# A float32 streaming-encoder step: the last four of sixteen chunks of x brought to feature layout by VectorE's 32x32 block transposes instead of TensorE products with the identity

## The chip, the cores and the metric

The kernel runs on one core of one Trainium2 chip. The metric is device time of the whole program in microseconds (us). Before the change it is 1937.66 us, the median of 3 runs (1937.37 to 1938.39). Every time below comes from those runs or from one profiled execution of the same program.

## What is computed

One layer of a hybrid encoder is run on 384 token rows of width 2048: 256 rows of one new stream (`x_prompt`) and 8 x 16 rows of running streams (`x_sample`). All data are float32. The part of the reference that the change touches is the first norm and the projection that follows it:

```python
def rmsnorm(x, g):
    xf = x.astype(jnp.float32)
    r = xf * lax.rsqrt(jnp.mean(xf * xf, axis=-1, keepdims=True) + EPS)
    return (r * g.astype(jnp.float32)).astype(x.dtype)
...
    h = rmsnorm(x, norm_mix_g)
    proj = h @ w_in
```

`proj` holds the values v, the queries, the keys, the forget logits, the input of a gated convolution branch and two gates. Attention, the convolution branch, an output projection and a feed-forward network with its own norm follow; the change touches none of them.

## The kernel before, in words

**Layout.** The 384 tokens are three tiles of 128 (`NTT = 3`, `NT = 384`), the 2048 features sixteen chunks of 128. x is loaded with tokens on partitions into four tiles `xs[0..3]`, each with 512 features, that is four chunks. A product with `w_in` needs features on partitions, so every chunk c of x is turned into a 128 x 384 block of `hT[c // 4]`. TensorE works in float32 by splitting both operands into a high part (type fp32r) and a low part (the rest): each product is three matmuls, high x high, high x low, low x high (lines 318 to 320 in `gemm`, in that order: L319 reads the low part of the weights, L320 the low part of x).

**Turning a chunk (`x_chunk`, L371 to 379).** TensorE multiplies three 128 x 128 tiles with the identity into one PSUM tile called misc (L374). ScalarE writes the high part of hT from it, scaled by the norm's weight g (L378), and VectorE writes the low part, g times x minus the high part (L379). The factor of the norm that belongs to a token, `rs1`, isn't applied here; it scales the products when they leave PSUM (`tok_evac`, L530 to 537).

**Weights.** `ahead` (L252) keeps two or three units of weights ready. A unit is 256 rows of w_in by up to 512 columns. SyncE's queue starts its DMA into one of three tiles `raw` (L157), ScalarE casts the high part `hi` (L176), VectorE subtracts to get the low part `lo` (L177). A `raw` tile is free for the next fetch only when VectorE's subtraction has read it, so SyncE's next fetch waits for `lo`. In this stage the same queue also starts the loads of x, two chunks at a time (L116, L118).

**The stage of the change.** The first product is for v: `gemm([(v_jobs[0], v_jobs[2])], [norm_steps])`, L542. It goes through the sixteen chunks in eight pairs. For a pair, job 0 uses one unit of weights (344 columns) for chunk c and then c + 1, and job 1 uses the next unit for the same two chunks: 4 x 9 matmuls a pair. After each nine matmuls `tick` advances a side generator, `first_norm` (L478). It calls `x_chunk` for the two chunks of the next pair, after the second and the third of the four ticks, and after each fourth chunk it has ScalarE sum the squares of one `xs` tile (L489, three instructions with the name junk). After the last of these sums VectorE and ScalarE work out `rs1` in a chain of ten small instructions (L500 to 503 and L127 to 132). Then the accumulators of v leave PSUM (L535), which frees the PSUM banks for the next product, the queries.

**What sets the order.** TensorE's order is written out by hand. On the other engines instructions go in the order that the scheduler chose by priority when the program was built: weights (`SPLIT_AHEAD`) and evictions (`EVAC_AHEAD`) go ahead of what has no priority, and `queued` keeps these among themselves in the order of the calls. Each engine then executes its list strictly in order.

Of the kernel before, what the change touches and what calls it, by code (L numbers as in the profile page):

```python
# [8 lines left out]
F32 = mybir.dt.float32  # L9
F32R = mybir.dt.float32r  # L10
AF = mybir.ActivationFunctionType
ALU = mybir.AluOpType
# [3 lines left out]
P = 128  # L16
DM = 2048
NT = 384
# [8 lines left out]
O_A, O_B, O_Q, O_K, O_V, O_GA, O_GB = 0, 1024, 2048, 3072, 4096, 5128, 7176  # L27

ATT_FIRST = 5
CONV_FIRST, CONV_LAG = 24, 17  # L30
LN_LAG = 0
SQ_LAG = 1
# [9 lines left out]
def hybrid_step(  # L42
# [9 lines left out]
    nc = tc.nc  # L52

    def pool(name, side="left", bufs=1, space=None):
        kw = dict(name=name, bufs=bufs, reuse_waits="tile")
        if space is not None:
            kw["space"] = space
        else:
            kw["side"] = side
        cm = tc.tile_pool(**kw)  # L60
        p = cm.__enter__()
        return p, lambda: cm.__exit__(None, None, None)
# [15 lines left out]
    def misc_tile():  # L78
        made[1] += 1
        return misc.tile([P, 512], F32, tag="misc", name="misc")  # L80
# [9 lines left out]
    def f(ap):  # L90
        return ap.bitcast(F32)
# [4 lines left out]
    stt = nc.vector.scalar_tensor_tensor  # L96
# [3 lines left out]
    p_x0, close_x0 = pool("x0", side="left")  # L100
    xs = [p_x0.tile([P, NTT, 512], F32, name=f"xs{n}") for n in range(4)]
# [4 lines left out]
    def queued(d, chain=True):  # L106
        e = d.ins.engine
        if chain and e in newest:
            tc.add_manual_dep(d.ins, newest[e], mybir.DependencyInfo(
                mybir.DependencyClass.NoSync, mybir.DependencyReason.DATA), reason="queue")  # L110
        newest[e] = d.ins.name
# [22 lines left out]
    def rsqrt(m, shape, p, tag):  # L134
        s = p.tile(shape, F32, tag=tag + "s", name=tag + "s")
        r = p.tile(shape, F32, tag=tag + "r", name=tag + "r")
        newton_rsqrt(r[:], s[:], m)
        return r
# [24 lines left out]
    def split_tiles():  # L163
        if banks and wide[0]:
            wide[0] += 1
            if wide[0] % 4 == 1:
                return res["wide"]()
        if extra and len(plan) > after_glu + 2:
            turns[0] += 1
            if turns[0] % 4 == 0:  # L170
                return [extra[0].tile([P, 2, 512], F32R, tag=tag, bufs=1, name=tag) for tag in ("hi", "lo")]
        return [wp.tile([P, 2, 512], F32R, tag=tag, bufs=3, name=tag) for tag in ("hi", "lo")]
# [177 lines left out]
    def by_feature(dst):  # L350
        return lambda a, js: dst[js].rearrange("p m (t a i) -> p m t a i", t=NTT, a=4)[:, :, :, a]
# [12 lines left out]
    hT = [gp.tile([P, 2, 4, NT], F32R, tag=f"G{g}", name=f"hT{g}") for g in range(4)]  # L364

    gm = cp.tile([P, 16], F32, name="gm")
# [4 lines left out]
    def x_chunk(c):  # L371
        ps = misc_tile()
        for t in range(NTT):
            tr(ps[:, t * P:(t + 1) * P], xs[c // 4][:, t, c % 4 * P:(c % 4 + 1) * P], ident[:])  # L374
        g = gm[:, c:c + 1]
        hi, lo = hT[c // 4][:, 0, c % 4, :], hT[c // 4][:, 1, c % 4, :]
        with tc.high_priority(offset=EVAC_AHEAD):
            queued(nc.scalar.activation(hi, ps[:, :NT], AF.Identity, scale=g))  # L378
            queued(stt(lo, ps[:, :NT], g, f(hi), op0=ALU.mult, op1=ALU.subtract))  # L379

    pe_order = tc.manual_schedule(engines={ENG.PE})
    pe_order.__enter__()
    with tc.manual_schedule(engines={ENG.SP, ENG.Activation, ENG.DVE}):
# [20 lines left out]
        hi, lo = split_tiles()  # L404
# [10 lines left out]
    def diagonals(dg, r):  # L415
        for t in range(NTT):
            ts(dg[:, t, :], ident[:], r[:, t:t + 1], None, op0=ALU.mult)
        return dg

    def over_partitions(dg, dst):  # L420
        ps = misc_tile()
        for t in range(NTT):
            mm(ps[:, t * P:(t + 1) * P], ones[:], dg[:, t, :], start=True, stop=True)
        nc.scalar.copy(dst, ps[:, :NT])
# [47 lines left out]
    def small_columns():  # L472
        ps = misc_tile()
        tr(ps[:, :R_N], vrow[:R_N, :], ident[:R_N, :R_N])
        nc.vector.tensor_copy(col[:], ps[:, :R_N])
        ts(qgs[:], col[:, R_QG:R_QG + 1], float(P) ** -0.5, None, op0=ALU.mult)

    def first_norm():  # L478
        for c in range(2, 16, 2):
            if c == 2:  # L480
                yield
            yield
            x_chunk(c)
            yield
            x_chunk(c + 1)
            if c % 4 == 2:
                for t in range(NTT):
                    n = c // 4
                    sq = nc.scalar.activation(junk[:], xs[n][:, t, :], AF.Square, accum_out=ssx[:, t, n:n + 1])  # L489
                    if c == 14:  # L490
                        queued(sq)
                    else:
                        tc.keep_in_program_order(sq)
            if c < 14:
                yield
            if 2 < c < 14:
                yield
        mt = p_x0.tile([P, NTT], F32, name="mt")
        with tc.high_priority(offset=EVAC_AHEAD):
            nc.vector.tensor_reduce(mt[:], ssx[:], axis=mybir.AxisListType.X, op=ALU.add)  # L500
            ts(mt[:], mt[:], 1.0 / DM, EPS, op0=ALU.mult, op1=ALU.add)
            r = rsqrt(mt[:], [P, NTT], p_x0, "r1")
            nc.vector.tensor_copy(rs1[:], r[:])
        for _ in range(14):
            yield
        small_columns()
        yield
        dg = diagonals(p_x0.tile([P, NTT, P], F32, name="r1d"), rs1)
        yield
        yield  # L510
        over_partitions(dg, rs1b[:])
        yield
# [26 lines left out]
    ha = grouped(hT)  # L539
    v_jobs = [job("B", 16, ha, tok_evac(vt, 344 * i, 344, shared=i == 2), n=344) for i in range(3)]  # L540
    norm_steps = first_norm()
    gemm([(v_jobs[0], v_jobs[2])], [norm_steps])  # L542

# [215 lines left out]
    def attention():  # L759
        at = {}  # L760
        for d in heads:
            for off, step in ((1, head_operands), (4, head_scores), (9, head_probs),
                              (12, head_out), (14, head_last)):
                at[ATT_FIRST + 6 * d["h"] + off] = step, d
        for t in range(max(at) + 1):
# [108 lines left out]
    for h in range(H):  # L874
        hi, lo = aHL[h // 4][:, 0, h % 4, :], aHL[h // 4][:, 1, h % 4, :]
# [710 lines left out]
    for n in (2, 3):  # L1586
        t = gp.tile([P, 2, 4, NT], F32R, tag=f"G{5 - n}", name=f"late{n}")
# [79 lines left out]
```

## Time and profile before

| | before |
|---|---|
| median of 3 runs | 1937.66 us |
| the profiled execution | 1938.61 us |
| its span, first to last instruction | 1936.9 us |
| TensorE busy in it | 1928.4 us |
| VectorE busy | 1556.1 us |
| ScalarE busy | 932.5 us |
| granted TensorE clock | 1.00 |

Time zero is the first instruction. The profiled execution took 1938.61 us, 1.7 us more than its span; it stands 0.95 us above the median. PE is TensorE's matmul part and PEld its weight load, which overlaps it; DVE is VectorE, ACT ScalarE, POOL GpSimd, SPq the DMA queue of SyncE. A row of a timeline reads: start, duration, engine, line, operation, output<-inputs, shapes, count, and in brackets the idle time ahead of it and what ended that.

### The profile page before, as it was taken

Reading aid. Unit: us, or ns where it says so; the run is one execution under the profiler, and the core shown is the slowest. Engines: PE = TensorE matmul, PEld = TensorE weight load, DVE = VectorE, ACT = ScalarE, POOL = GpSimd, SP = SyncE. Lnnn points to the kernel's source line nnn. Section 1 sums busy time; section 2 is a strip of 40 time slices with the busy share of each in tenths; the row PEclk is TensorE's granted clock in tenths of the full one; section 3 lists DMA queues with packets and bytes.
Section 4 is the critical chain, followed back from the end, with each engine's and each line's share of the span. In section 5 each row is a group of like instructions: output and inputs, shape, how many; then the busy total and the mean of one; then the engine's idle time right before and its main releaser. Section 6 shows DMA issues by size and latency. Waiting matters only on the chain.

```text
span 1936.9 us, 25423 instructions
## 1 busy us (share of the span) xinstructions
PE 1928.4 (100%) x9132; PEld 1629.3 (84%) x9132; DVE 1556.1 (80%) x2131; ACT 932.5 (48%) x1322; POOL 151.0 (8%) x298
## 2 busy tenths in 40 slices
PE   9999999999999999999999999999999999999999
PEld 9888999988888888888888888888888888888887
DVE  4446979888864568677699989898999999999985
ACT  5444454433333522344556464555555555555552
POOL 2000001100000000000101010101010101101010
PEclk9999999999999999999999999999999999999999
DMA  6564677454444343634545454545454545545453
GB/s 185 156 184 119 211 166 167 136 148 126 132 132 130 121 130 129 205 124 130 154 147 164 145 164 149 153 152 162 133 164 151 165 152 155 166 139 177 134 162 138
DMA packets 220721, 293.37 MB, mean 151 GB/s; under 512 B 59354, under 2 KB 105109, under 8 KB 220587
## 3 DMA queue, kind: packets, MB, share of 16 engines
q1 hardware_dynamic: 213395, 281.74, 49.1%
q0 software_dynamic: 7168, 10.00, 2.0%
q8 instruction: 71, 1.16, 0.3%
q14 instruction: 55, 0.45, 0.1%
q10 hardware_dynamic: 32, 0.01, 0.0%
HBM read 266.98 MB, written 7.86 MB: 142 GB/s over the span
## 4 chain that ended last, share of the span: by engine, by line
PE 96%; DVE 2%; DMA 1%; issue 0%; SPq 0%; ACT 0%; ACTq 0%; DVEq 0%
PE bank L1412 17%; PE bank L1411 17%; PE bank L1410 17%; PE acc L320 8%; PE acc L318 8%; PE acc L319 8%; PE misc L320 4%; PE misc L318 4%; PE misc L319 4%; PE acc L313 2%; PE acc L315 2%; PE acc L314 2%; DMA raw<-in_w_down_dram 0%; DVE mixT L337 0%; DVE lo L177 0%
## 5 line engine op out<-in xcount | busy, mean ns | idle before, releaser
L1103 ACT CAST hi<-raw 128x1024 fp32r<-128x1024 f32 x260 | 270.3, 1051 | 316.1 <-DVE raw L1103 140.3
L177 DVE TENSOR_TENSOR lo<-raw,hi 128x1024 fp32r<-128x1024 f32 (+2 forms) x219 | 259.5, 1187 | 194.7 <-ACT hi L176 192.5
L176 ACT CAST hi<-raw 128x1024 fp32r<-128x1024 f32 (+2 forms) x219 | 221.7, 1012 | 387.9 <-PE misc L320 300.6
L1103 DVE TENSOR_TENSOR lo<-raw,hi 128x1024 fp32r<-128x1024 f32 x260 | 314.7, 1221 | 48.2 <-ACT hi L1103 46.5
L318 PE MATMUL acc<-hi,hT 128*128 128x512 f32 (+1 forms) x512 | 193.1, 377 | 1.3 <-ACT hT L378 1.3
L320 PE MATMUL acc<-hi,hT 128*128 128x512 f32 (+1 forms) x512 | 190.5, 372 | 0.1
L319 PE MATMUL acc<-lo,hT 128*128 128x512 f32 (+1 forms) x512 | 190.1, 371 | 0.0
L1410 PE MATMUL bank<-hi,xg 128*128 128x512 f32 x440 | 171.2, 389 | 0.0
L1411 PE MATMUL bank<-lo,xg 128*128 128x512 f32 x440 | 171.2, 389 | 0.0
L1412 PE MATMUL bank<-hi,xg 128*128 128x512 f32 x440 | 171.2, 389 | 0.0
L835 DVE SCALAR_TENSOR_TENSOR ut<-ext,cw,ut 128x384 f32<-128x384 f32 x240 | 151.2, 630 | 6.0
L1412 PE MATMUL bank<-hi,act 128*128 128x512 f32 x396 | 154.2, 389 | 0.2 <-DVE act L1103 0.2
L1410 PE MATMUL bank<-hi,act 128*128 128x512 f32 x396 | 154.1, 389 | 0.0
L1411 PE MATMUL bank<-lo,act 128*128 128x512 f32 x396 | 154.0, 389 | 0.0
L1103 ACT CAST x21h<-raw 128x1024 fp32r<-128x1024 f32 x82 | 86.2, 1051 | 101.7 <-DVE raw L1103 50.1
L318 PEld LDWEIGHTS acc<-hi,hT 128*128 128x128 f32 x512 | 96.3, 188 | 16.6 <-ACT hT L378 1.6
L320 PEld LDWEIGHTS acc<-hi,hT 128*128 128x128 f32 x512 | 96.1, 188 | 15.5 <-DVE hT L379 0.5
L319 PEld LDWEIGHTS acc<-lo,hT 128*128 128x128 f32 x512 | 96.4, 188 | 14.9
L1103 DVE TENSOR_TENSOR x21l<-raw,x21h 128x1024 fp32r<-128x1024 f32 x82 | 100.2, 1222 | 7.8 <-ACT x21h L1103 6.7
L1411 PEld LDWEIGHTS bank<-lo,xg 128*128 128x128 f32 x440 | 82.6, 188 | 17.1
L1410 PEld LDWEIGHTS bank<-hi,xg 128*128 128x128 f32 x440 | 82.6, 188 | 17.1
L1412 PEld LDWEIGHTS bank<-hi,xg 128*128 128x128 f32 x440 | 82.6, 188 | 17.1
(393 smaller groups left out, 4277.1 us busy)
## 6 DMA issues: line engine op xcount, KB each, us to landing
raw<-in_w_up_dram SPq DMA_DIRECT2D x176, 512.0 KB
raw<-in_w_in_dram SPq DMA_DIRECT2D x96, 512.0 KB
raw<-in_w_down_dram SPq DMA_DIRECT2D x88, 512.0 KB
raw<-in_w_in_dram SPq DMA_DIRECT2D x64, 256.0 KB
raw<-in_w_out_dram SPq DMA_DIRECT2D x32, 512.0 KB
raw<-in_w_att_out_dram SPq DMA_DIRECT2D x16, 512.0 KB
raw<-in_conv_pw_out_dram SPq DMA_DIRECT2D x16, 512.0 KB
raw<-in_w_in_dram SPq DMA_DIRECT2D x23, 344.0 KB
```

The source lines that it names most:

```text
L176: queued(nc.scalar.copy(hi[:, k, :o], raw[:, k, :o]), first)
L177: queued(tt(lo[:, k, :o], raw[:, k, :o], f(hi[:, k, :o]), op=ALU.subtract), first)
L313: mm(o, hi[:, kk, s], ah, start=st, stop=False)
L314: mm(o, hi[:, kk, s], al, start=False, stop=False)
L318: mm(o, ah[:, s], hi[:, kk, :n], start=st, stop=False)
L319: mm(o, ah[:, s], lo[:, kk, :n], start=False, stop=False)
L320: mm(o, al[:, s], hi[:, kk, :n], start=False, stop=sp)
L835: stt(o, v, wc, o, op0=ALU.mult, op1=ALU.add)
L1103: d = op(*args, **kw)
L1410: mm(o, ah, h[:, kk, :], start=start, stop=False, **kw)
L1411: mm(o, ah, l[:, kk, :], start=False, stop=False, **kw)
L1412: mm(o, al, h[:, kk, :], start=False, stop=stop, **kw)
```

## The change

For chunks 12 to 15 `x_chunk` isn't called any more. Instead `x_pair(c)` is called for c = 12 and c = 14, one tick earlier than `x_chunk(c)` was. It has VectorE transpose the two chunks in blocks of 32 x 32 straight from `xs` into a new SBUF tile `xT`: 16 instructions a pair, each reading 32 partitions and writing 32 partitions, with 2 chunks x 3 token tiles x 32 = 192 elements a partition. ScalarE and VectorE then write the high and low part of hT as before, with `xT` in place of the PSUM tile as input. These two are still `queued`, but no longer under `EVAC_AHEAD`, and the transposes have no priority either. The removed matmuls are 4 chunks x 3 = 12.

```diff
@@ -27,6 +27,7 @@
 ATT_FIRST = 5
+X_PAIRS = 12
 CONV_FIRST, CONV_LAG = 24, 17
@@ -377,6 +378,19 @@
+    def x_pair(c):
+        xT = p_x0.tile([P, 2, NT], F32, tag="xT", bufs=2, name="xT")
+        o = c % 4 * P
+        src = xs[c // 4][:, :, o:o + 2 * P].rearrange("p t (m b j) -> p b m t j", m=2, b=4)
+        for b in range(4):
+            for a in range(4):
+                nc.vector.transpose(by_feature(xT)(a, slice(32 * b, 32 * b + 32)), src[32 * a:32 * a + 32, b])
+        for m in range(2):
+            g = gm[:, c + m:c + m + 1]
+            hi, lo = hT[c // 4][:, 0, c % 4 + m, :], hT[c // 4][:, 1, c % 4 + m, :]
+            queued(nc.scalar.activation(hi, xT[:, m], AF.Identity, scale=g))
+            queued(stt(lo, xT[:, m], g, f(hi), op0=ALU.mult, op1=ALU.subtract))
@@ -479,10 +493,14 @@
         for c in range(2, 16, 2):
             if c == 2:
                 yield
+            if c >= X_PAIRS:
+                x_pair(c)
             yield
-            x_chunk(c)
+            if c < X_PAIRS:
+                x_chunk(c)
             yield
-            x_chunk(c + 1)
+            if c < X_PAIRS:
+                x_chunk(c + 1)
             if c % 4 == 2:
```

The lists of the engines that the two programs were built to show what this moves. On TensorE only the twelve matmuls are gone; on SyncE and GpSimd nothing moves. Behind the stretch shown the lists are the same on all engines, but for one small instruction of VectorE that trades places with a weight subtraction. Line numbers of the changed program are larger by 1 up to the end of `x_chunk`, by 14 up to the calls of `x_chunk` in `first_norm` and by 18 behind them.

First place, VectorE, from the low part of chunk 9 on (`lo_...` are low parts of weights, `hT2` holds chunks 8 to 11, `hT3` chunks 12 to 15). Before:

```order
L379 SCALAR_TENSOR_TENSOR hT2_87<-misc_438,gm_89,hT2_87 128x384
L177 TENSOR_TENSOR lo_458<-raw_455,hi_457 128x2x344
L379 SCALAR_TENSOR_TENSOR hT2_87<-misc_479,gm_89,hT2_87 128x384
L177 TENSOR_TENSOR lo_488<-raw_485,hi_487 128x2x344
L379 SCALAR_TENSOR_TENSOR hT2_87<-misc_500,gm_89,hT2_87 128x384
L177 TENSOR_TENSOR lo_523<-raw_520,hi_522 128x2x344
```

After:

```order
L388 STREAM_TRANSPOSE xT_535<-xs3_79 32x6x32 x2
L380 SCALAR_TENSOR_TENSOR hT2_87<-misc_438,gm_89,hT2_87 128x384
L178 TENSOR_TENSOR lo_458<-raw_455,hi_457 128x2x344
L388 STREAM_TRANSPOSE xT_535<-xs3_79 32x6x32 x12
L380 SCALAR_TENSOR_TENSOR hT2_87<-misc_479,gm_89,hT2_87 128x384
L178 TENSOR_TENSOR lo_488<-raw_485,hi_487 128x2x344
L388 STREAM_TRANSPOSE xT_535<-xs3_79 32x6x32
L380 SCALAR_TENSOR_TENSOR hT2_87<-misc_500,gm_89,hT2_87 128x384
```

The first sixteen transposes stand between the low parts of chunks 9 to 11, twelve of them in one block ahead of the low part of chunk 10 and of `lo_488`; the sixteenth follows the last row shown.

Second place, VectorE, from there to the start of the `rs1` chain. Before:

```order
L379 SCALAR_TENSOR_TENSOR hT3_88<-misc_544,gm_89,hT3_88 128x384
L177 TENSOR_TENSOR lo_553<-raw_550,hi_552 128x2x344
L379 SCALAR_TENSOR_TENSOR hT3_88<-misc_565,gm_89,hT3_88 128x384
L177 TENSOR_TENSOR lo_585<-raw_582,hi_584 128x2x344
L177 TENSOR_TENSOR lo_591<-raw_588,hi_590 128x2x344
L379 SCALAR_TENSOR_TENSOR hT3_88<-misc_612,gm_89,hT3_88 128x384
L177 TENSOR_TENSOR lo_621<-raw_618,hi_620 128x2x344
L379 SCALAR_TENSOR_TENSOR hT3_88<-misc_633,gm_89,hT3_88 128x384
```

After:

```order
L388 STREAM_TRANSPOSE xT_612<-xs3_79 32x6x32
L178 TENSOR_TENSOR lo_568<-raw_565,hi_567 128x2x344
L388 STREAM_TRANSPOSE xT_612<-xs3_79 32x6x32 x2
L178 TENSOR_TENSOR lo_594<-raw_591,hi_593 128x2x344
L388 STREAM_TRANSPOSE xT_612<-xs3_79 32x6x32 x6
L178 TENSOR_TENSOR lo_600<-raw_597,hi_599 128x2x344
L388 STREAM_TRANSPOSE xT_612<-xs3_79 32x6x32 x4
L393 SCALAR_TENSOR_TENSOR hT3_88<-xT_612,gm_89,hT3_88 128x384 x2
L178 TENSOR_TENSOR lo_645<-raw_642,hi_644 128x2x344
```

The sixteen transposes of the second pair are mixed with three weight subtractions (the same three as `lo_553`, `lo_585` and `lo_591` before; their numbers changed); the first three of them stand between the rows of the first place and these. The low parts of chunks 14 and 15 now come last but one, behind all 32 transposes.

Third place, ScalarE, the same stretch (`junk` are the sums of squares). Before:

```order
L176 CAST hi_590<-raw_588 128x2x344
L378 ACTIVATE hT3_88<-misc_612,gm_89 128x384
L176 CAST hi_620<-raw_618 128x2x344
L378 ACTIVATE hT3_88<-misc_633,gm_89 128x384
L489 ACTIVATE junk_92,ssx_91<-xs3_79 128x512 x3
L127 ACT_TABLE_LOAD
```

After:

```order
L177 CAST hi_599<-raw_597 128x2x344
L392 ACTIVATE hT3_88<-xT_612,gm_89 128x384 x2
L177 CAST hi_644<-raw_642 128x2x344
L507 ACTIVATE junk_92,ssx_91<-xs3_79 128x512 x3
L128 ACT_TABLE_LOAD
```

The high parts of chunks 14 and 15 stand together now, they wait for VectorE's last transpose, and the cast of a weight unit and the sums of squares that `rs1` needs stand behind them.

## The prediction

> **What bounds the kernel now.** First the page's shares and its chain of work that ended last, then the idle time of TensorE by what ended it:
>
> ```profile
> span 1936.9 us, 25423 instructions
> PE 1928.4 (100%) x9132; PEld 1629.3 (84%) x9132; DVE 1556.1 (80%) x2131; ACT 932.5 (48%) x1322; POOL 151.0 (8%) x298
> ...
> PE 96%; DVE 2%; DMA 1%; issue 0%; SPq 0%; ACT 0%; ACTq 0%; DVEq 0%
> ```
>
> ```profile
> PE misc L398 <- POOL ident L123: 1.5, 1, 1.5
> PE acc L318 <- ACT hT L378: 1.3, 1, 1.3
> PE misc L966 <- DVE sgA L960: 0.5, 2, 0.3
> ```
>
> TensorE bounds the kernel from end to end. Its longest waits are over by 10 us of 1937, and behind them none is longer than 0.3 us. So a microsecond taken off TensorE's stream is a microsecond gained, a microsecond that it newly waits is one lost, and nothing later takes it back. Next the stretch of the change, from the windows of busy time:
>
> ```profile
> 33.15:54.15 21.00, 21.00 (x140) 20.89 (x139) 10.46 (x14) 12.20 (x25) 0.00 (x0) 1.00 0.61 168
> ```
>
> The columns are length, then busy time and count of PE, PEld, DVE, ACT and POOL, then the granted clock. TensorE has no gap in these 21.00 us; VectorE is busy for 10.46 and has 10.54 to spare.
>
> **What the change removes.** Two of the removed turns in TensorE's timeline, with the start of the product pair ahead of them:
>
> ```profile
> 40.23 0.32 PE L318 MATMUL acc<-hi,hT 128*128 128x344 f32 x1
> ...
> 43.07 0.49 PE L374 MATMUL misc<-ident,xs 128*128 128x128 f32 x3
> ...
> 44.81 0.49 PE L374 MATMUL misc<-ident,xs 128*128 128x128 f32 x3
> ```
>
> From 40.23 to 43.07 stand eighteen matmuls of 344 columns: 2.84 / 18 = 0.158 us from start to start. From 43.07 to 44.81 stand one turn and nine such matmuls: 1.74 - 9 x 0.158 = 0.32 us for a turn. Four turns are gone: **-1.29 us**, if everything else holds.
>
> **What it adds.** 32 transposes of 192 elements a partition. The profile has transposes of 384 on 32 partitions, and of 256 on 128:
>
> ```profile
> L337 DVE STREAM_TRANSPOSE attT<-qt 32x384 f32<-32x384 f32 x32 | 18.2, 570 | 0.5
> ...
> L812 DVE STREAM_TRANSPOSE ext<-sc 128x256 f32<-128x256 f32 x8 | 3.5, 439 | 1.8 <-DMA sc<-in_state_conv_dram 1.7
> ```
>
> ```profile
> 146.50 3.49 DVE L337 STREAM_TRANSPOSE attT<-qt 32x384 f32<-32x384 f32 x6
> 150.02 1.23 DVE L177 TENSOR_TENSOR lo<-raw,hi 128x1024 fp32r<-128x1024 f32 x1
> 151.28 4.09 DVE L337 STREAM_TRANSPOSE attT<-qt 32x384 f32<-32x384 f32 x7
> ```
>
> 128 elements fewer cost 131 ns less, so 64 fewer than 256 should cost 65 less: 439 - 65 = 374 ns. Six in a row take 3.49 us, (3.49 - 0.57) / 5 = 0.584 from start to start, 0.014 of it gap. I take **0.384 us** apiece, 12.29 us in all. The bounds are 0.285 (half of 570, no fixed cost) and 0.584 (the wider one's spacing, no saving by width). The form of the access is that of L337 with half the blocks, so I stay near the straight line.
>
> 12.29 us are more than the 10.54 us to spare. So VectorE must become the bound for a while, and the sum has to follow its list. These rows give where it starts and the other two kinds in it:
>
> ```profile
> 31.54 0.62 DVE L379 SCALAR_TENSOR_TENSOR hT<-misc,gm,hT 128x384 fp32r<-128x384 f32 x1 [3.06 <-ACT hT L378]
> 32.20 0.88 DVE L177 TENSOR_TENSOR lo<-raw,hi 128x688 fp32r<-128x688 f32 x1
> 33.29 0.62 DVE L379 SCALAR_TENSOR_TENSOR hT<-misc,gm,hT 128x384 fp32r<-128x384 f32 x1 [0.22 <-ACT hT L378]
> ```
>
> The first transposes take the place of the 0.22 us wait after the row at 32.20, at 32.20 + 0.88 + 0.03 (the gap seen above ahead of 151.28) = 33.11. By the new order these stand up to the last transpose: 32 transposes (12.29), the low parts of chunks 9 to 13, five at 0.66 (31.54 to 32.20), 3.30, and six weight subtractions at 0.88 + 0.03, 5.46. Sum 21.05, so the last transpose ends at **54.16**, if VectorE never waits in between. Its inputs allow that: the high parts of chunks 9 to 11 come from TensorE turns that end before VectorE gets to them, and x for chunks 12 and 13 has landed, since DMA traffic stops by 33.0:
>
> ```profile
> 32.00:32.50 0.50, 0.50 (x6) 0.48 (x6) 0.46 (x2) 0.17 (x1) 0.00 (x0) 1.00 0.33 113
> 32.50:33.00 0.50, 0.50 (x6) 0.50 (x5) 0.50 (x1) 0.33 (x1) 0.00 (x0) 1.00 0.03 10
> 33.00:33.50 0.50, 0.50 (x5) 0.50 (x4) 0.28 (x2) 0.50 (x2) 0.00 (x0) 1.00 0.00 0
> ```
>
> (The last two columns are DMA share and GB/s.) Were the transfer late after all, the waiting transpose would hold up all of VectorE's list, one for one.
>
> **The added wait and what queues behind it.** ScalarE's high parts of chunks 14 and 15 wait for that last transpose. Behind them on ScalarE stand a weight cast and the three sums of squares, behind those `rs1`, behind `rs1` VectorE's subtraction for the first unit of the query product, and for that TensorE waits. How this ran before:
>
> ```profile
> 15.44 0.76 ACT L176 CAST hi<-raw 128x688 fp32r<-128x688 f32 x1
> 16.09 0.63 ACT L489 ACTIVATE junk<-xs 128x512 f32<-128x512 f32 x1
> ...
> 51.67 0.58 ACT L378 ACTIVATE hT<-misc,gm 128x384 fp32r<-128x384 f32 x1 [0.51 <-PE misc L374]
> 52.15 0.62 ACT L489 ACTIVATE junk<-xs 128x512 f32<-128x512 f32 x1
> ```
>
> ```profile
> 56.93 0.17 DVE L503 COPY rs<-r1r 128x3 f32<-128x3 f32 x1
> 57.42 1.23 DVE L177 TENSOR_TENSOR lo<-raw,hi 128x1024 fp32r<-128x1024 f32 x1 [0.32 <-issue]
> ```
>
> ```profile
> 58.58 0.40 PE L318 MATMUL acc<-hi,hT 128*128 128x512 f32 x1
> 58.81 0.40 PE L319 MATMUL acc<-lo,hT 128*128 128x512 f32 x1
> ```
>
> The first sum started at 52.15; the subtraction ended at 57.42 + 1.23 = 58.65; the query product's second matmul, which reads its result, started at 58.81. The cover before was 58.81 - 58.65 = 0.16 us, of which I allow 0.05 for the signal. Now: 54.16, signal 0.04, two high parts at 0.48 (51.67 to 52.15) give 55.16, the cast 0.65 (15.44 to 16.09) gives 55.81 for the first sum, 6.50 later (58.65 - 52.15) the subtraction ends at 62.31, and TensorE's second matmul starts at 62.36 instead of 58.81: **+3.55 us**. The high parts read SBUF now; the cast's 0.65 for 688 elements there makes me expect a little under 0.48, so I take **+3.5**.
>
> The 1.29 us saved lie inside this: without waits the query product would start early, so TensorE must wait about 3.5 + 1.3 = 4.8 us in all. It does so piecewise, and the pieces don't add to the sum. The first, by this row,
>
> ```profile
> 40.39 0.32 PE L319 MATMUL acc<-lo,hT 128*128 128x344 f32 x1
> ```
>
> is at the first product of chunk 10, which reads `lo_488`. VectorE's list gives for it 33.11 + 2 x 0.384 + 0.66 + 0.91 + 12 x 0.384 + 0.66 + 0.88 = 41.60, so TensorE waits about 1.3 us at 40.39. More follow at chunk 12 (some 0.4), at chunk 14 (its high part ends near 54.8; some 1.8) and at the query product (the rest).
>
> SyncE's fetches wait for VectorE's subtractions, so they slip by 2 us and more. They have cover:
>
> ```profile
> 39.44 2.11 SPq L157 DMA_DIRECT2D raw<-in_w_in_dram  x2
> ```
>
> ```profile
> 45.82 0.76 ACT L176 CAST hi<-raw 128x688 fp32r<-128x688 f32 x1
> ```
>
> The fetch issued at 39.44 was cast at 45.82, 6.4 us later, with no wait for DMA. It will now be issued near 41.6, and the cast moves to about 46.2 behind the new high parts: 4.6 us are left. I cost the fetches at nothing; if the cover were gone, VectorE's list would stop for what is missing.
>
> Behind the query product's start the lists are as before and all engines are late by the same 3.5 us. Against the profiled execution's 1938.61 (span 1936.9) this gives 1942.1; that execution stands 0.95 above the median of 1937.66, from which I count: 1937.66 + 3.5 = **1941.2**.
>
> **A rule that speaks otherwise.** The rows above price twelve 128 x 128 tiles at 12.29 us of VectorE, 1.02 each, against 1.29 / 12 = 0.11 on TensorE. The Trainium skill, "VectorE: DVE Perf Modes", section "The three transpose paths", puts a 128 x 128 bf16 tile at 311 ns on VectorE and 390 on TensorE, blocks of 32 only. By its 311 ns the estimate would be 12 x 0.311 = 3.7 us of VectorE, well inside the 10.54 to spare, and only the saving would be left. The trace agrees with that figure for an instruction on 128 partitions (the L812 row less 128 elements gives 439 - 131 = 308 ns), but the change's instructions fill 32 partitions each, a quarter, so its price per tile doesn't hold here. Its section "Rules for kernel authors" says to use TensorE for 128 x 128 if PSUM will do.
>
> **The rivals.**
>
> *Hidden after all.* If a transpose takes the lower bound, 0.285 us, the list shortens by 32 x 0.099 = 3.2 us, and the sum is about +0.3. Below some 0.23 us VectorE is never late and the full saving stays: 1937.66 - 1.29 = 1936.4. For it speaks that VectorE idles for half of the stretch; against it that the rows of 256 and 384 elements both carry a fixed part of some 175 ns (439 - 256 x 1.023, 570 - 384 x 1.023). Chance of +1.5 us or less 0.11.
>
> *Slower by more than a measurement's doubt.* 0.2%, 3.9 us, is about what a measurement of this kernel can tell from no change. While VectorE is the bound each transpose counts 32 times: 0.01 us more makes 0.32 us. The point that decides is 0.384 + (3.9 - 3.5) / 32 = 0.396 us. At 0.42, plausible if short rows at 32 partitions cost more than a straight line, the sum is +4.7, 1942.3. At the upper bound of 0.584 it is 3.5 + 32 x 0.2 = 9.9, 1947.6. A late x transfer, or SBUF shared with ScalarE's reads of the same `xs`, would act in the same place. The point is near, so its chance is 0.38.
>
> *The clock.* TensorE gets gaps of 1 to 2 us. The profile has one of 1.3 us, and the clock there stays at 1.00:
>
> ```profile
> 9.39 0.42 PE L318 MATMUL acc<-hi,hT 128*128 128x344 f32 x1 [1.31 <-ACT hT L378]
> ```
>
> ```profile
> 0.00:20.00 20.00, 17.08 (x98) 16.04 (x99) 7.30 (x13) 9.86 (x19) 9.02 (x31) 1.00 0.78 215
> ```
>
> Should the clock halve for one unit of eighteen matmuls, that costs another 2.84 us: 1944.0. Chance 0.04. The Trainium skill, "TensorE: Matmul & The Clock Gate", section "Part 1: The HAM clock gate", has the clock drop after an idle window of about 3.4 us. By that rule our gaps are too short.
>
> *The change doesn't do what it says.* The built lists show the twelve matmuls gone and the 32 transposes in place, so this has next to no chance.
>
> **How the numbers follow.** The forecast, between +1.5 and +3.9 us, gets 0.47, slower by one of the two mechanisms 0.42, hidden 0.11, of which 0.03 would be over 0.2% faster, by something that I don't see. Faster 0.03, within 0.2% 0.55, slower 0.42. The range leaves out about a tenth at each end: from 1937.8 (a transpose near its lower bound) to 1944.5 (0.49 us each, or the clock). The likeliest case's own range is 1939.2 to 1941.5.
>
> **What would show it.** Right: VectorE without a gap from about 33 to 54 us; transposes near 0.37 us; TensorE waiting for `lo` at about 40.4 us, for hT at about 53 and for `lo` or `rs` at about 61; the query product near 62. Wrong: gaps in VectorE's row there (then something else holds the end); transposes at 0.29 or at 0.45; a first transpose waiting for a DMA; a clock below 1.00; or TensorE waits behind 70 us that were not there before.

## The result: 2.9 us slower, and the profile after

| | before | after |
|---|---|---|
| median of 21 runs each | 1937.89 us | 1940.81 us |
| lowest to highest | 1937.12 to 1938.75 | 1939.83 to 1943.24 |
| ratio after / before, 95% interval | | 1.0015 (1.0009 to 1.0021) |
| profiled execution, its span | 1938.61, 1936.9 us | 1940.94, 1939.2 us |
| granted clock | 1.00 | 1.00 |

The change made the kernel 2.9 us slower (1.7 to 4.1 by the interval). The forecast was +3.5 us and 1941.2 us. By the medians that is 0.15%, in the terms of the prediction "within 0.2%"; the interval reaches just past that, to 0.21%.

First the waits of TensorE in the profile after, largest first (total, times, longest):

```profile
PE misc L412 <- POOL ident L124: 1.5, 1, 1.5
PE acc L319 <- ACT hT L392: 1.3, 1, 1.3
PE acc L320 <- DVE lo L178: 0.9, 1, 0.9
PE misc L984 <- DVE sgA L978: 0.5, 2, 0.3
PE acc L319 <- ACT vt L553: 0.4, 1, 0.4
PE acc L319 <- ACT hT L379: 0.4, 1, 0.4
```

Three of the six are new: hT from L392 (the high part of chunk 14), a weight's low part, and vt, the eviction of v that needs `rs1`. The first and the fourth were there before; the last is the one at the start of the program, 1.3 us before. Behind 70 us nothing is new. The window of the change and the new group of instructions:

```profile
33.15:54.15 21.00, 18.80 (x119) 18.03 (x117) 19.58 (x44) 8.74 (x18) 0.00 (x0) 1.00 0.49 139
```

```profile
L388 DVE STREAM_TRANSPOSE xT<-xs 32x192 f32<-32x192 f32 x32 | 11.8, 370 | 0.6
```

TensorE, full before, now lacks 2.20 of the 21.00 us; VectorE went from 10.46 to 19.58, and what is left of its time there is the gaps between instructions and one wait at the end. A transpose takes 370 ns. VectorE's timeline, at the two places that count:

```profile
32.93 0.75 DVE L388 STREAM_TRANSPOSE xT<-xs 32x192 f32<-32x192 f32 x2
33.71 0.62 DVE L380 SCALAR_TENSOR_TENSOR hT<-misc,gm,hT 128x384 fp32r<-128x384 f32 x1
34.25 0.86 DVE L178 TENSOR_TENSOR lo<-raw,hi 128x688 fp32r<-128x688 f32 x1
35.14 4.59 DVE L388 STREAM_TRANSPOSE xT<-xs 32x192 f32<-32x192 f32 x12
39.76 0.62 DVE L380 SCALAR_TENSOR_TENSOR hT<-misc,gm,hT 128x384 fp32r<-128x384 f32 x1
40.30 0.87 DVE L178 TENSOR_TENSOR lo<-raw,hi 128x688 fp32r<-128x688 f32 x1
...
51.93 1.53 DVE L388 STREAM_TRANSPOSE xT<-xs 32x192 f32<-32x192 f32 x4
54.14 1.15 DVE L393 SCALAR_TENSOR_TENSOR hT<-xT,gm,hT 128x384 fp32r<-128x384 f32 x2 [0.68 <-ACT hT L392]
...
59.96 0.17 DVE L521 COPY rs<-r1r 128x3 f32<-128x3 f32 x1
60.04 1.23 DVE L178 TENSOR_TENSOR lo<-raw,hi 128x1024 fp32r<-128x1024 f32 x1
```

From 32.93 to 53.46 (51.93 + 1.53) VectorE runs without a wait: that is the stretch in which it is the bound. ScalarE picks up at once, and its sums of squares stand behind:

```profile
53.49 1.12 ACT L392 ACTIVATE hT<-xT,gm 128x384 fp32r<-128x384 f32 x2 [5.69 <-DVE xT L388]
54.52 0.75 ACT L177 CAST hi<-raw 128x688 fp32r<-128x688 f32 x1
55.18 0.63 ACT L507 ACTIVATE junk<-xs 128x512 f32<-128x512 f32 x1
```

And TensorE, with the turn of chunk 9 as a mark ahead of the change's stretch:

```profile
31.94 0.49 PE L375 MATMUL misc<-ident,xs 128*128 128x128 f32 x3
...
40.02 0.32 PE L319 MATMUL acc<-hi,hT 128*128 128x344 f32 x1
41.22 0.42 PE L320 MATMUL acc<-lo,hT 128*128 128x344 f32 x1 [0.88 <-DVE lo L178]
41.48 0.32 PE L321 MATMUL acc<-hi,hT 128*128 128x344 f32 x1
...
52.51 0.32 PE L321 MATMUL misc<-hi,hT 128*128 128x344 f32 x1
54.16 0.43 PE L319 MATMUL acc<-hi,hT 128*128 128x344 f32 x1 [1.34 <-ACT hT L392]
54.42 0.32 PE L320 MATMUL acc<-lo,hT 128*128 128x344 f32 x1
54.82 0.42 PE L321 MATMUL acc<-hi,hT 128*128 128x344 f32 x1
...
60.13 0.32 PE L321 MATMUL misc<-hi,hT 128*128 128x344 f32 x1
60.83 0.49 PE L319 MATMUL acc<-hi,hT 128*128 128x512 f32 x1 [0.38 <-ACT vt L553]
61.32 0.50 PE L320 MATMUL acc<-lo,hT 128*128 128x512 f32 x1
```

The same mark in the profile before:

```profile
32.15 0.49 PE L374 MATMUL misc<-ident,xs 128*128 128x128 f32 x3
```

**How the traces are compared.** Executions differ by some 2 us ahead of this mark, from the start of the program (it comes at 31.20 us in e2 and at 33.34 in e1). So I measure from the turn of chunk 9 to the query product's second matmul: 58.81 - 32.15 = 26.66 us before, 61.32 - 31.94 = 29.38 after, **+2.72 us**. All experiments below are given by this distance too. Each distance comes from one execution; what an experiment doesn't touch can differ by some 0.15 us between two of them (chunk 10 in e3 is an example).

**Where TensorE lost it.** Undisturbed matmuls of 344 columns start every 0.158 us, those of 512 every 0.23. What a start is later than that is lost, and this sum is larger than the listed idle time:

| place | predicted wait | listed idle | lost by the starts |
|---|---|---|---|
| chunk 10, `lo` (40.02 to 41.48) | 1.3 | 0.88 | 1.04 + 0.10 |
| chunk 12 (near 47 us) | 0.4 | none | 0.14 |
| chunk 14, hT (52.51 to 55.08) | 1.8 | 1.34 | 1.49 + 0.10 + 0.24 + 0.10 |
| query product (60.13 to 61.32) | 1.3 | 0.38 | 0.54 + 0.26 |
| sum | 4.8 | 2.6 | 4.0 |

4.0 lost less 1.29 saved is 2.7, the distance measured.

### The profile page after: what moved, and what is told of

Same layout as the page of the kernel before. It is cut to its first block, busy times and chain, and to the rows that moved or that the text cites. A ratio compares the mean times of both kernels' runs of the same rounds, so it can differ in the third digit from the quotient of the medians.

```text
span 1939.2 us, 25432 instructions
## 1 busy us (share of the span) xinstructions
PE 1929.1 (99%) x9120; PEld 1628.5 (84%) x9120; DVE 1567.0 (81%) x2163; ACT 932.3 (48%) x1322; POOL 150.8 (8%) x298
## 4 chain that ended last, share of the span: by engine, by line
PE 96%; DVE 2%; issue 0%; ACT 0%; DMA 0%; SPq 0%; DVEq 0%; ACTq 0%
PE bank L1430 18%; PE bank L1428 18%; PE bank L1429 18%; PE acc L320 8%; PE acc L319 8%; PE acc L321 8%; PE misc L321 4%; PE misc L320 4%; PE misc L319 4%; PE acc L314 2%; PE acc L316 2%; PE acc L315 2%; DVE lo L178 1%; DVE mixT L338 0%; DVE xT L388 0%
```

## The experiments

**The theories.** *Load*: 32 transposes of 0.38 us don't fit into VectorE's spare time before chunk 14 is due, so everything behind them in its list is late. *Lost precedence*: the new hand-over (transposes without priority, high and low parts without `EVAC_AHEAD`, SBUF in place of PSUM) costs the time, whatever the transposes take. *Tail*: only the sums of squares matter, which are stuck on ScalarE behind the last transpose. All times are medians of 11 runs; their comparison is with runs of the kernel before on the same chip, 1938.19 us for e1 to e4 (33 runs), 1938.43 for e5 to e8 (33 runs), 1938.20 for e9 (15 runs).

**e1: the change without its transposes.** Left out are the 32 transposes; chunks 12 to 15 of hT hold x unturned (`src` is the chunk in `xs`, `three` splits a row of 384 into its three tiles).

```diff
-                nc.vector.transpose(by_feature(xT)(a, slice(32 * b, 32 * b + 32)), src[32 * a:32 * a + 32, b])
...
-            queued(nc.scalar.activation(hi, xT[:, m], AF.Identity, scale=g))
-            queued(stt(lo, xT[:, m], g, f(hi), op0=ALU.mult, op1=ALU.subtract))
+            queued(nc.scalar.activation(three(hi), src, AF.Identity, scale=g))
+            queued(stt(three(lo), src, g, three(f(hi)), op0=ALU.mult, op1=ALU.subtract))
```

> Left out: the 32 transposes; hT of chunks 12 to 15 is made from x as it lies, so these chunks hold untransposed values. The twelve TensorE matmuls are gone as in the change. Theory (load): VectorE has less free time between the landing of x and the moments at which its results are due than 32 narrow transposes take, so without them no wait is left and only the saved turns remain: -1.3 us against before, 1936.6, and the query product's second matmul near 57.5 us. Rival (handover): the cost comes from the new input in SBUF and from the evictions that lost their precedence, not from the transposes: then TensorE still waits at chunk 14 and behind it, and the time stays within 1 us of the changed kernel's 1940.8. Rival (no saving): the turns were worth nothing; then 1937.9.

Measured: 1937.01 us, ratio 0.9995 (0.9986 to 1.0004). By the mark (chunk 9 at 33.34, the matmul at 58.69) the distance is 25.35, -1.31 us: the whole price of four turns, with no new wait of TensorE in the stage. By its time alone e1 can't be told from the kernel before; it is clearly faster than the change. Without the transposes the hand-over costs nothing: the loss comes with the transposes.

**e2: eight wide transposes in place of 32 narrow ones.** Each runs over 128 partitions. Left out is the exchange of blocks between the four groups of 32 partitions.

```diff
-            for a in range(4):
-                nc.vector.transpose(by_feature(xT)(a, slice(32 * b, 32 * b + 32)), src[32 * a:32 * a + 32, b])
+            nc.vector.transpose(by_feature(xT)(b, slice(0, P)), src[:, b])
```

> The 32 transposes on 32 partitions become 8 on 128 partitions of the same 192 elements, which leaves out the moves of blocks between groups of 32 partitions (so chunks 12 to 15 hold blocks in the wrong places). Everything else is as in the change. Theory (load): one instruction takes the same 0.37 us whatever its partitions, so VectorE needs 8 x 0.38 = 3.1 us in place of 12.2 and is never late: -1.3 us against before, 1936.6, as with no transposes at all. Rival (price per tile): if four times the partitions cost more, say 0.7 us apiece, 5.6 us still fit and the time says little, but the rows show it. Rival (handover): TensorE waits for hT of chunk 14 as in the change, 1940 to 1941.

Measured: 1937.20 us, ratio 0.9995 (0.9986 to 1.0004), distance 56.55 - 31.20 = 25.35, -1.31. The form's row of min, median and max duration:

```profile
L387 DVE STREAM_TRANSPOSE xT<-xs x8: 335/371/378, 32.0 to 41.6; 128x192 f32<-128x192 f32 x8
```

Four times the partitions at the same price: 371 ns against 370. A quarter of VectorE's time for the same bytes, and the loss is gone. Together with e1 this is what load says, and lost precedence falls: the list still has transposes without priority here, in the same kind of places.

**e3: the last sums of squares ahead of the high parts of chunks 14 and 15.** Nothing is left out; `squares(c)` is the loop over the three sums, called for c = 14 ahead of `x_pair(14)`.

```diff
+            if c == 14:
+                squares(c)
             if c >= X_PAIRS:
                 x_pair(c)
...
-            if c % 4 == 2:
+            if c % 4 == 2 and c < 14:
+                squares(c)
```

> Nothing is left out. The three sums of squares over the last x tile stand ahead of the high parts of chunks 14 and 15 on ScalarE, so the norm's factor no longer waits for three sums behind the last transpose; the table load and root still stand behind those high parts and one weight cast. Theory (load): the waits at chunks 10 and 14, 0.9 + 1.3 + 0.4 us in the changed kernel's trace, stay, the wait at the query product, some 0.8 us, goes: 0.8 us less than the changed kernel, about 1940.0. Rival (the tail alone sets the end, as the prediction summed it): with 2.25 us taken from it, 2.2 us less, 1938.6. Rival (handover): no change, 1940.8.

Measured: 1939.94 us, ratio 1.0011 (1.0002 to 1.0020), distance 60.02 - 31.62 = 28.40, +1.74. TensorE's waits that concern the stage:

```profile
PE acc L319 <- ACT hT L392: 1.3, 1, 1.3
...
PE acc L320 <- DVE lo L178: 0.7, 1, 0.7
```

The wait for vt at the query product is gone; the other two are still there, 1.3 and 0.7 against 1.3 and 0.9. The distance is 2.72 - 1.74 = 0.98 us shorter. Of this the tail is worth 0.80, what TensorE lost at the query product in the table; the other 0.18 is lost less at chunks 10 and 12, which the edit doesn't touch (the first transposes started 0.80 us behind the start of the subtraction ahead of them here, 0.94 in the change). The rest is lost earlier. The tail alone falls as the cause; it is one of three places.

**e4: the same number of transposes, spread.** Pairs 10 and 14 go through VectorE in place of 12 and 14.

```diff
-X_PAIRS = 12
+X_PAIRS = (10, 14)
```

The tests for the pair become `c in X_PAIRS`, here and in what follows.

> Nothing is left out. The pairs turned by VectorE are chunks 10, 11 and 14, 15 instead of 12 to 15, so as many transposes are spread over twice the time; the built list puts twelve of the first sixteen in one block and all sixteen of the second in one block, each ahead of a weight subtraction that TensorE needs next. Theory (load alone counts): 6.1 us in each 12.7 us of the stage fit into VectorE's idle half; no waits, -1.3 us, 1936.6. Rival (queueing in order): a block of 12 takes 4.6 us and one of 16 takes 6.1 us, more than the 3 us or so by which the weights' low parts are ahead; TensorE waits about 1.2 us for the low part of weights near 34 us and 2 to 3 us near 46 us, less the 1.3 saved: +2 us, about 1940.

Measured: 1942.33 us, ratio 1.0019 (1.0010 to 1.0028), distance 63.33 - 32.22 = 31.11, +4.45. Spreading made it worse, so load over the whole stretch isn't all. VectorE's list and TensorE's waiting matmul:

```profile
42.66 6.12 DVE L388 STREAM_TRANSPOSE xT<-xs 32x192 f32<-32x192 f32 x16 [1.50 <-DMA xs<-in_x_sample_dram]
48.80 0.62 DVE L380 SCALAR_TENSOR_TENSOR hT<-misc,gm,hT 128x384 fp32r<-128x384 f32 x1
49.34 0.86 DVE L178 TENSOR_TENSOR lo<-raw,hi 128x688 fp32r<-128x688 f32 x1
```

```profile
46.97 0.32 PE L319 MATMUL acc<-hi,hT 128*128 128x344 f32 x1
50.26 0.42 PE L320 MATMUL acc<-lo,hT 128*128 128x344 f32 x1 [2.97 <-DVE lo L178]
```

All sixteen transposes of the pair stand in one block here, the block waits 1.50 us for its x, and a weight subtraction that TensorE needs at 47 us stands behind it. Without the wait for x this list would be 1.50 us ahead, so by this sum about half of the 2.97 us is the order and half the late x. At pair 10 the block of twelve waits for nothing, and TensorE still lost 0.98 us behind it (a listed wait of 0.71 at 34.99 us). The order of VectorE's list is a cause of its own: **a block in front of something urgent delays it by the block's whole length**, and TensorE waits for what the spare time ahead of it doesn't cover. And behind the gap of 2.97 us came a second loss, seen in the granted clock (column behind POOL):

```profile
48.50:50.00 1.50, 0.00 (x0) 0.00 (x0) 1.47 (x3) 1.12 (x2) 0.00 (x0) 1.00 0.00 0
50.00:51.50 1.50, 1.24 (x7) 1.25 (x8) 1.50 (x4) 0.00 (x0) 0.00 (x0) 0.91 0.16 23
51.50:53.00 1.50, 1.50 (x7) 1.50 (x6) 1.50 (x4) 0.00 (x0) 0.00 (x0) 0.50 0.83 228
53.00:54.50 1.50, 1.50 (x6) 1.50 (x6) 0.36 (x1) 0.00 (x0) 0.00 (x0) 0.50 0.87 261
54.50:56.00 1.50, 1.50 (x11) 1.50 (x11) 0.45 (x1) 1.25 (x3) 0.00 (x0) 0.95 1.05 389
```

At a clock of 0.50 matmuls start every 0.285 us; eleven of them lost 0.127 each, 1.4 us. So of the 5.7 us that TensorE lost in this execution of e4 the clock took a quarter. Over the whole program the granted clock is recorded as 0.999 in six of e4's eleven executions, this one among them, and as 1.000 in five; their medians are 1942.60 and 1941.24 us, 1.36 apart. That fits a drop which comes in some executions and not in others; only the profiled one was read.

**e5: pairs 10 and 14 again, but paced.** The transposes stand in VectorE's list in pieces of nine and seven with weight subtractions between them, x of these pairs is loaded a pair earlier, and the sums stand ahead as in e3. `paced` calls a generator form of `x_pair` from the side.

```diff
+    X_LOADS = {13: [4], 11: [6], 9: [8, 10], 5: [12, 14]}
...
-                if x_left and (len(plan) - v_last) in range(3, 14, 2):
-                    load_x(x_left.pop(0), 2)
+                for c in X_LOADS.get(len(plan) - v_last, ()):
+                    load_x(c, 2)
...
+            for _ in range({8: 4, 15: 2}.get(n, 0)):
+                yield
...
-    gemm([(v_jobs[0], v_jobs[2])], [norm_steps])
+    gemm([(v_jobs[0], v_jobs[2])], [paced(), norm_steps])
```

> Pairs 10 and 14 go through VectorE, as in e4, but their transposes stand in VectorE's list in pieces of nine and seven with weight subtractions between them, their x is loaded a pair earlier, and the last sums of squares stand ahead. If both load and queueing decide (what e4 suggests), no TensorE wait for a weight subtraction is above 1 us, the clock stays at 1.00, and the time is 1936.9 to 1938.2 (the saving of 1.29 less what small waits remain). If load alone decided, e4 would have been as fast, and this kernel would repeat e4's 1942. If transposes at chunk 14 are bound to end late whatever their place, a wait of 1 us or more stays for hT of chunk 14 and the time is 1938.5 to 1940.

Measured: 1938.01 us, ratio 0.9998 (0.9990 to 1.0007), distance 58.18 - 31.71 = 26.47, -0.19. The clock stays at 1.00, and no wait for a weight is left. The only wait in the stage:

```profile
PE acc L321 <- DVE hT L394: 0.5, 2, 0.3
```

It is for the low parts of chunks 14 and 15, and by the starts of the matmuls it costs 1.1 us, which leaves 0.2 of the 1.29 saved. Part of it comes from the order that I gave: the low part of chunk 15 stands behind the `rs1` chain.

```profile
51.28 0.61 DVE L394 SCALAR_TENSOR_TENSOR hT<-xT,gm,hT 128x384 fp32r<-128x384 f32 x1
53.16 0.18 DVE L129 RECIPROCAL r1r<-r1s 128x3 f32<-128x3 f32 x1 [1.27 <-ACT r1s L128]
53.26 0.59 DVE L394 SCALAR_TENSOR_TENSOR hT<-xT,gm,hT 128x384 fp32r<-128x384 f32 x1
```

From e4 to e5 the distance fell by 4.6 us with the same 32 transposes. Three edits went together; they weren't tried apart, so how much each brought stays open. Pairs 12 and 14, those of the change, weren't tried paced.

**e6: only pair 10, eight transposes in each of two idle places of VectorE.** As e5, but the sums of squares stay in their old place, and these lines differ:

```diff
-X_PAIRS = (10, 14)
+X_PAIRS = (10,)
-    X_LOADS = {13: [4], 11: [6], 9: [8, 10], 5: [12, 14]}
+    X_LOADS = {13: [4], 11: [6], 9: [8, 10], 5: [12], 3: [14]}
-            for _ in range({8: 4, 15: 2}.get(n, 0)):
+            for _ in range({7: 4, 15: 2}.get(n, 0)):
```

> Only the pair 10 goes through VectorE, eight transposes (3.06 us) in each of two places of its list, with x of that pair loaded earlier; chunks 12 to 15 are turned on TensorE as before the change. Load theory with queueing: the two turns' 0.64 us are saved and nothing waits, 1937.0 to 1937.8. If taking turns off TensorE brings nothing in itself (the moves wait elsewhere), 1937.8 to 1938.3. If a block of 3.06 us is already too long for a due subtraction, 1938.5 or more, with the wait at one of chunks 8 to 11.

Measured: 1937.76 us, ratio 0.9996 (0.9987 to 1.0005), distance 57.52 - 31.51 = 26.01, -0.65, two turns at 0.32. TensorE doesn't wait once between the mark and the query product. A turn on VectorE is free in this stage when its pieces fit between two due subtractions. Whether the program keeps the gain isn't shown: in this execution TensorE waits 1.57 us for VectorE's tile `act` near the end of the program, at 1900.17 us, where before it waited 0.18, and its time, 1938.67 us, is the longest of the eleven. What makes that wait longer wasn't followed.

**e7: only pair 14, as the change has it.** 16 transposes, 6.1 us, against 10.5 to spare.

```diff
-X_PAIRS = 12
+X_PAIRS = (14,)
```

> Only the last pair (chunks 14 and 15) goes through VectorE, as the change has it: 16 transposes, 6.1 us, well under the 10.5 us that VectorE had to spare. Load theory alone: two turns saved, 0.64 us, no wait for hT or lo above 0.3 us, 1937.2 to 1937.7. Load and queueing: a block of 12 transposes, 4.59 us, stands ahead of chunk 12's low part and of a weight subtraction, which come about 1.2 us late; 0.6 us worse than before in sum, 1938.2 to 1938.9, with the wait at the second products of chunks 12 or 13 and none at the query product.

Measured: 1939.83 us, ratio 1.0009 (1.0000 to 1.0018), distance 60.18 - 32.66 = 27.52, +0.86. VectorE, then TensorE:

```profile
42.56 4.59 DVE L388 STREAM_TRANSPOSE xT<-xs 32x192 f32<-32x192 f32 x12
47.18 0.62 DVE L380 SCALAR_TENSOR_TENSOR hT<-misc,gm,hT 128x384 fp32r<-128x384 f32 x1
47.72 0.86 DVE L178 TENSOR_TENSOR lo<-raw,hi 128x688 fp32r<-128x688 f32 x1
```

```profile
47.07 0.32 PE L319 MATMUL acc<-hi,hT 128*128 128x344 f32 x1
48.63 0.43 PE L320 MATMUL acc<-lo,hT 128*128 128x344 f32 x1 [1.24 <-DVE lo L178]
```

Half the load, well inside the spare time, and still a loss: -0.64 saved, 1.40 + 0.11 lost at this one place, +0.87 in all. Part of the wait is the pair's x, for which the first two transposes waited:

```profile
40.35 0.75 DVE L388 STREAM_TRANSPOSE xT<-xs 32x192 f32<-32x192 f32 x2 [0.44 <-DMA xs<-in_x_sample_dram]
```

From there to the subtraction VectorE doesn't wait again, so with x in time some 0.8 of the 1.24 us would stay, by this sum still a loss. This tells queueing from load. The median is 1.40 above that of before and lies above the range that I expected. What exceeds the 0.86 isn't explained. The profiled execution has 0.28 us more of a wait far behind the stage, for `act` at 1901.69 us (0.46, before 0.18).

**e8: the early loads of x alone.** All turns on TensorE, x fetched as in e5.

```diff
-X_PAIRS = 12
+X_PAIRS = ()
```

> All turns on TensorE as before the change, but x of chunks 10 to 15 is fetched one pair earlier, as e5 has it: what the fetches alone do. Expected without effect, 1937.7 to 1938.4. If earlier fetches crowd the weight stripes, the first products of the gate stage wait, and e5 and e6 carry that cost too.

Measured: 1938.59 us, ratio 1.0001 (0.9992 to 1.0010), distance 58.64 - 31.97 = 26.67, +0.01. The fetches do nothing by themselves.

**e9: pairs 6 and 10, paced like e6.** The attempt at a version better than both, with four turns off TensorE and the tail left alone.

```diff
-X_PAIRS = (10,)
+X_PAIRS = (6, 10)
-    X_LOADS = {13: [4], 11: [6], 9: [8, 10], 5: [12], 3: [14]}
+    X_LOADS = {13: [4, 6], 9: [8, 10], 5: [12], 3: [14]}
```

> Pairs 6 and 10 go through VectorE, eight transposes (3.06 us) in each of four idle places of its list, x of pair 6 fetched a pair earlier too; chunks 12 to 15 stay on TensorE. As many turns leave TensorE as in the change (four), as many transposes are added (32). If load against room and place decide, twice e6: the query product's second matmul 1.3 us earlier than before against the turn of chunk 9, but for what the turn of pair 6 saves ahead of that mark (0.65 of it lies before), no TensorE wait, 1936.9 to 1937.6 at a median of 1938.2 for before. If x of pair 6 comes too late for its transposes, a wait at chunks 6 and 7 of some 1 us and 1938 or more. If 32 narrow transposes cost what they do wherever they stand, 1940 or more.

Measured: 1938.23 us, ratio 1.0000 (0.9991 to 1.0009), distance 58.80 - 32.80 = 26.00, -0.66: pair 10 pays as in e6. But the mark itself came 0.65 us later than before where it should have come 0.65 earlier, and TensorE waits ahead of it that e6 doesn't have:

```profile
PE acc L320 <- DVE lo L178: 0.5, 1, 0.5
...
PE acc L319 <- ACT hT L379: 0.5, 2, 0.2
...
PE misc L375 <- DMA xs<-in_x_prompt_dram: 0.2, 1, 0.2
```

The first is for a weight at 22.57 us behind a piece of eight transposes, 0.78 by the starts, which is more than the 0.64 that the two turns of pair 6 save. The expectation missed: pair 6 gives nothing at this place. The waits for hT (8.01 and 14.65 us) and for x (11.97 us, the turn of chunk 2) lie ahead of it; e1, which fetches x as the change does, has such waits at the same places. How much of the rest is the start of the program, which differs between executions, isn't separated.

No version beat the kernel before by more than the measurement can tell. e1 and e2 show the ceiling: -1.3 us, 0.07%, if all four turns were free.

## Why the prediction was right, point by point

- **The saving, -1.29 us: right.** e1 and e2 give -1.31 by the mark, e6 gives -0.65 for two turns.
- **The price of a transpose, 0.384 us from start to start: right.** Twelve in a row take 4.59 us, (4.59 - 0.37) / 11 = 0.384. The straight line through the rows of 256 and 384 elements held at 192. With that the rival "hidden after all" and the rival of dearer transposes, which decided at 0.396, both fell, the second by a narrow margin (the interval of the medians, up to 4.1 us, doesn't quite exclude its 3.9; the distance of 2.72 does for the profiled execution).
- **VectorE becomes the bound, its list ends at 54.16: right in kind, 0.5 us too late.** The end was 53.46, or 53.67 in the time of before (the mark stands 0.21 earlier). The transposes fit; what was mis-sized are the rows between them. I had 0.66 for a low part and 0.91 for a subtraction. In this full list the next instruction starts 0.54 to 0.64 us behind a low part (33.71 to 34.25 is the shortest) and 0.79 to 0.91 behind a subtraction: 2.92 in place of 3.30 for five, 5.29 in place of 5.46 for six.
- **ScalarE behind the last transpose: right.** First sum at 55.18, 1.72 behind the last transpose, where I had 55.81 - 54.16 = 1.65. The high parts were expected a little under 0.48; the two took 0.52 each (53.49 to 54.52).
- **The tail of 6.50 us from the first sum to the end of the subtraction: 0.4 too long.** It took 61.27 - 55.18 = 6.09. Before, the subtraction had started 0.49 us behind the copy of `rs`, with 0.32 us idle for which the profile names no releaser; now it starts 0.08 behind (59.96 to 60.04). I counted this idle time as work of the chain. It isn't part of it: e8, whose turns are those of before, has it again (57.24 us, 0.32 idle), and e1, in which nothing is late, hasn't (0.08). What causes it stays open. The end of the chain was as summed: the query product's second matmul starts 0.05 us behind the end of the subtraction (61.27 to 61.32).
- **These two terms are the error.** In the time of after the first sum was predicted for 55.81 - 0.21 = 55.60 and came 0.42 earlier; the tail was 0.41 shorter; 3.55 - 0.83 = 2.72, the distance measured. The step that was off is the same in both: gaps of before were carried into a list in which they don't recur. Both errors made the forecast too high. The time itself, 1941.2 against 1940.81, came closer than this by luck: the base of 3 runs, 1937.66, lies 0.23 below the median of 21.
- **TensorE's waits come piecewise, 4.8 us in all: right in place, 4.0 in size**, as the table above has it. The first was said to be 1.3 at the first product of chunk 10 and cost 1.14 there; at chunk 14 it was 1.8 and cost 1.93; the query product took up the rest. There the listed wait is for vt at the first matmul; `lo` or `rs` was named. The second matmul does wait for `lo`, but the list shows no idle time ahead of it.
- **Fetches at nothing: right.** VectorE waits for no DMA in the stretch of the change. It isn't so wherever the transposes stand: they waited for their x in e7 (0.44 us) and e4 (1.50).
- **The clock: right for the change in the profiled execution, at 1.00.** But its rival was real: e4 has it.
- **Cause, wider than I had it.** The prediction's working follows VectorE's list in order, and so it had the right waits; its words were that 12.29 us don't fit into 10.54. e7 shows that this isn't needed: 6.1 us in 10.5 lose as well when twelve of the sixteen transposes stand ahead of a due subtraction. And e6 shows that sixteen such transposes are free in their stage between two due ones.

## What to carry to other kernels

Spare time of an engine over a stretch says little; what counts is what stands behind the new work in that engine's list, and when it is due. Work moved to an idle engine goes into its idle places in pieces that fit between two due instructions, and not behind the last input of the stage, where a chain (here the sums, `rs1`, the evictions) hangs on it. When such a list is summed for a prediction, take the spacing under load and leave out waits that belonged to the old order.

## What the runs showed of the hardware

- A 32 x 32 block transpose of 192 elements a partition takes 370 ns on 32 partitions and 371 on 128. The same bytes on a quarter of the partitions take four instructions, and so four times the time.
- A wait costs TensorE more than its listed idle time. At 41.22 us 0.88 us are listed; the start is 1.04 late, since the row ahead is shown 0.32 long where the next would have started after 0.158, and the first matmul after the break holds up the next by another 0.10 (0.42 long, 0.26 from start to start). Some 0.26 us for each break come on top.
- After a gap of 2.97 us (3.13 by the starts), the clock in e4's profiled execution fell to 0.50. Slow matmuls start at 51.15, 0.9 us after TensorE is back at work, and go on to 54.51, 3.4 us. Gaps of up to 1.34 us in the change left it at 1.00, and so did one of 1.57 us in e6. The Trainium skill, "TensorE: Matmul & The Clock Gate", section "Part 1: The HAM clock gate", has the clock drop after an idle window of about 3.4 us; the length of the slow stretch agrees with that window, while the drop here followed 2.97 us of listed idle time.
